# An MLP's value weights, loaded across the border of two column groups

## The chip, the core and the metric

The kernel runs on one core of a Trainium2 chip. The metric is the device time of one execution in microseconds (us). Before the change it is 1210.47 us, the median of three runs (1209.59 to 1212.47). TensorE (PE in the profile) multiplies matrices, VectorE (DVE) and ScalarE (ACT) work on elements, GpSimd (POOL) hardly matters here, and SyncE (SP) issues most of the loads from HBM.

## What is computed

Two layers of a decoder trunk on 512 tokens of width 1024, in float32. The first has sliding-window attention and a short gated convolution, the second gated linear attention; both end with the same gated MLP and a per-layer embedding. The change is in the MLP:

```python
D_MODEL, SEQ, D_FF, FFN_CONV_K = 1024, 512, 2816, 3
def _conv_ffn(h, w_up, conv_w, conv_b, w_down):
    u = _causal_depthwise_conv(h @ w_up, conv_w) + conv_b
    gate, up = jnp.split(u, 2, axis=-1)
    return (jax.nn.gelu(gate, approximate=False) * up) @ w_down
```

`w_up` has 2 x 2816 columns: the first half makes the gate, the second half the values that the gate multiplies.

## The kernel before

The matmuls run on pairs of numbers. Each float32 operand is split into a rounded part (`wh`, ScalarE) and the rest (`wl`, VectorE), and three products (lines 169 to 171, or 878 to 880) take the place of one. This split is called a cut: `cut` (lines 149 and 150) for plain weights, `cut_blocks` (lines 825 and 826) for weights that are used in blocks.

The up-projection `h @ w_up` of a layer runs in 11 groups. Group d makes two columns of 128 gate features and two columns of 128 value features, for all 512 tokens. The two halves are computed in different ways:

- The **gate columns** 256d to 256d + 255 go through `seven`: a scheme of seven half-size block products in the place of eight. Its weights are the plain blocks, sums and differences of blocks that VectorE forms in place in the loaded buffer (lines 849 to 860), each cut in turn. The last cut that reads the buffer is `last = self.cut_blocks(od)`. `seven` is a generator: each `next(steps)` issues some products and returns after a small copy between PSUM tiles, line 899 and line 902 among them.
- The **value columns** are plain products of three matmuls each (`value`, 48 matmuls a column), each with a cut of its own (`column`).

The weights come from HBM into two buffers of one pool (tag `raw`, 1 MB each, `bufs=2`). A load can only be issued when the cuts that read the buffer's former content are done. In `prepare(d)`, `loaded(d)` issues both loads of group d on SP's queue: first 256 value columns, then 256 gate columns. Then the second value column (`w1`) is cut, then the gate forms, and then the first value column.

TensorE's order is written out by hand. Group d begins with 36 matmuls of the column that was cut first (`begin`), goes on with products of the gate, mixed with the other value column (`V0`), and while its last gate products run, `prepare(d + 1)` is already recorded. Between L899 and L902 stands half a value column, and after L902 come the last two gate products, 24 matmuls, ahead of the next group. ScalarE and VectorE take their instructions in an order that a scheduler has fixed when the program was built, and each engine takes its own queue in that order. `tc.issue_after(x)` puts what is recorded inside it behind instruction x, where both are on one engine.

What VectorE does in a group besides the cuts: it scales the product by the tokens' norm (`z`, line 927, or 930 and 934) and adds two taps of the convolution (`zt`, line 937) for each of the four columns, and multiplies value and gate (line 982 or 992) after ScalarE's gelu (line 1077).

Of the kernel before, what the change touches and what calls it, by code (L numbers as in the profile page):

```python
# [19 lines left out]
P = 128  # L20
# [3 lines left out]
ND = D // P  # L24
DFF = 2816
NF = DFF // P
# [37 lines left out]
class Kernel:  # L64
# [291 lines left out]
    def project(self, load, ks, done, then):  # L356


        for m2 in range(0, ND, 2):
            pss = [self.ps(), self.ps()]  # L360
            raw = self.raw(ND, 2 * P)
            load(raw, slice(m2 * P, (m2 + 2) * P))
            w = self.cut(raw, "b")
            for c in range(2):
                for k in range(ND):
                    self.mm3(pss[c], w(k, c * P, (c + 1) * P), ks[k], start=k == 0, stop=k == ND - 1)
            if m2 + 2 == ND:
                then()
            for c in range(2):
                done(m2 + c, pss[c])  # L370
# [536 lines left out]
    def ffn(self, i, project, next_gain):  # L907


        nc, a, tc = self.nc, self.a, self.tc  # L910
        gain = self.g_ffn[i]
        wu = a["ffn_w_up"][i].rearrange("(k p) n -> p k n", p=P)
        w0, w1, w2, bb = self.fcv

        mine, other = (("a0", "a1"), ("b0", "b1"))[:: 1 - 2 * i]
        with tc.tile_pool(name=f"ffn{i}", bufs=1) as fp:
# [4 lines left out]
            def both():  # L921
                return fp.tile([P, 2, S], F32, tag="zt", name=self.nm("zt"), bufs=2)

            def taps(y, ps, f, more=None, behind=None):
                z = fp.tile([P, S], F32, tag="z", name=self.nm("z"), bufs=3)
                if more is None:
                    nc.vector.tensor_tensor(z, ps, R, ALU.mult)  # L927
                else:
                    h2 = lambda x: x.rearrange("p (u t) -> p u t", u=2)
                    nc.vector.tensor_tensor(  # L930
                        h2(z), h2(ps), more.unsqueeze(1).to_broadcast([P, 2, S // 2]), ALU.add
                    )
                    with tc.issue_after(behind.ins) if behind else nullcontext():
                        nc.vector.tensor_tensor(z, z, R, ALU.mult)  # L934
                nc.scalar.activation(y, z, AF.Identity, scale=w2[:, f : f + 1], bias=bb[:, f : f + 1])  # L935
                for tap, w in ((1, w1), (2, w0)):
                    nc.vector.scalar_tensor_tensor(  # L937
                        out=y[:, tap:], in0=z[:, : S - tap], scalar=w[:, f : f + 1], in1=y[:, tap:],
                        op0=ALU.mult, op1=ALU.add,
                    )  # L940

            def loaded(d):

                out = [self.raw(ND, 256) for _ in range(2)]
                for raw, c0 in zip(out, (DFF + 256 * d, 256 * d)):
                    nc.sync.dma_start(raw, wu[:, :, c0 : c0 + 256])
                return out

            def column(raw, c):
                return self.cut(raw[:, :, c * P : (c + 1) * P], "b", BLOCKS)  # L950

            def value(w, ps, k0, k1):
                for c, k in itertools.product(HALVES, range(k0, k1)):
                    self.mm3(
                        ps[:, c], w(k, 0, P), [x[:, c] for x in xg[k]], start=c.start == 0 and k == 0,
                        stop=k == ND - 1,
                        skip_group_check=True,
                    )

            def prepare(d):  # L960

                rv, rg = loaded(d)
                w1 = column(rv, 1)
                ev, od = self.by_parity(rg)
                ws = self.seven_forms(ev, od, rg)
                return self.seven(od, ws, xg, self.forms), w1, column(rv, 0)

            def begin(d, steps, w):

                ps = self.pa()  # L970
                value(w, ps, 0, 6)
                next(steps)
                value(w, ps, 6, ND)
                return lambda y: taps(y[:, 1], ps, NF + 2 * d + 1)

            def place(d, g, y):

                f = 2 * d
                if f < 8:
                    kept[f : f + 2] = [self.fp.tile([P, S], F32, tag=other[0], name=self.nm("u")) for _ in range(2)]  # L980
                    for u in range(2):
                        nc.vector.tensor_tensor(kept[f + u], g[:, u], y[:, u], ALU.mult)
                    return
                if d == groups - 1:
                    x = y
                else:
                    if f % 4 == 0:
                        fours.append(self.four(fp, F32))
                    x = fours[-1][:, f % 4 : f % 4 + 2]
                kept[f : f + 2] = [x[:, 0], x[:, 1]]  # L990
                pairs[f] = x
                nc.vector.tensor_tensor(x, g, y, ALU.mult)
# [3 lines left out]
            def split_one(f):  # L996

                tag = other[1 if f < 4 else 0]
                h = self.fp.tile([P, S], F32R, tag=tag, name=self.nm("uh"))
                pool, tag = (self.fp, tag) if f < 7 else (self.sp, "R")  # L1000
                acts[f] = h, pool.tile([P, S], F32R, tag=tag, name=self.nm("ul"))
                self.split(acts[f], kept[f])
# [6 lines left out]
            def split_acts():  # L1009
                for f in (6, 7):  # L1010
                    split_one(f)
# [24 lines left out]
            xg = self.xg  # L1036
            ready = []

            def done(m, ps):
                nc.vector.tensor_tensor(self.xT[m], self.xT[m], ps, ALU.add)  # L1040
                self.operand(m, gain, mine)

            project(done, lambda: ready.extend(prepare(0)))
            steps, w1c, w0c = ready
            with tc.manual_schedule(engines={ET.PE}):
                late = begin(0, steps, w1c)
                close = lambda: None
                for d in range(groups):
                    g, y = both(), both()
                    copied = next(steps)  # L1050
                    with tc.issue_after(copied.ins):
                        close()
                    V0 = self.pa()
                    value(w0c, V0, 0, ND // 2)
                    if d == 0:
                        self.end_norm()
                    copied = next(steps)
                    value(w0c, V0, ND // 2, ND)
                    if d == 0:
                        R = self.spread()  # L1060
                    X, Y, more = next(steps)
                    rest, cut = late, None

                    if d + 1 < groups:
                        steps, w1c, w0c = prepare(d + 1)
                        cut = self.rest_cut
                        late = begin(d + 1, steps, w1c)
                    else:
                        split_acts()
                    with tc.issue_after(copied.ins):  # L1070
                        rest(y)
                    taps(y[:, 0], V0, NF + 2 * d)
                    taps(g[:, 0], X, 2 * d)
                    taps(g[:, 1], Y, 2 * d + 1, more, cut)

                    def close(d=d, g=g, y=y):
                        nc.scalar.activation(g, g, AF.Gelu)
                        place(d, g, y)
                        if 4 <= d < groups - 1:
                            split_one(d - 4)  # L1080

                close()
# [910 lines left out]
```

## Time and profile before

| | us |
|---|---|
| median of the runs shown | 1210.47 (1209.59 to 1212.47) |
| the profiled execution, its own time | 1212.17 |
| its span in the profile | 1210.4 |
| up-projection of layer 0, groups 0 to 10 (first matmul to first of the down-projection) | 179.01 to 411.04 |
| up-projection of layer 1 | 802.69 to 1033.40 |

The times in a row of the profile are microseconds from the start of the span. A row in order of time has start, duration, engine, line, operation, output and inputs, shape; in brackets stands for how long the engine was idle before it and what ended that. A row of stretches begins with its bounds and its length, and gives each engine's busy time and instructions (PE, PEld, DVE, ACT, POOL), the granted clock, the share of the DMA engines and GB/s. A row of the chain has start, duration and what it was. The granted TensorE clock is 0.999 of full speed over the whole span.

### The profile page before, as it was taken

The numbers are of one execution on the slowest core, as the hardware profiler recorded it, in microseconds if no ns is written. First come the engines' busy times: TensorE is split into PE (matmuls) and PEld (weight loads), VectorE is DVE, ScalarE is ACT, GpSimd is POOL, SyncE is SP. The second block draws the span as 40 slices with busy tenths as digits, with TensorE's granted clock in tenths as the row PEclk, the third lists the DMA queues.
The fourth block names the chain that finished last, engine by engine and source line by source line (L and its number), as shares of the span: only waits on it lengthen the run. The fifth ranks groups of instructions, "written<-read, shape, count | busy, mean of one in ns | idle before, by whom it ended". The sixth has DMA issues, their size and how long they took to land.

```text
span 1210.4 us, 19832 instructions
## 1 busy us (share of the span) xinstructions
PE 1199.7 (99%) x8074; PEld 1080.0 (89%) x8074; DVE 968.3 (80%) x1543; ACT 667.0 (55%) x1093; POOL 45.1 (4%) x64
## 2 busy tenths in 40 slices
PE   9999999999999999999999999999999999999998
PEld 8877789999999989888988988899999999888887
DVE  6786687898998996746679876678988899988595
ACT  7466565655555744534563555555555656645374
POOL 2610000000000000000100000000000000000000
PEclk9999999999999999999999999999999999999999
DMA  7232222424233243222322222322242423422601
GB/s 221 72 103 72 73 70 71 139 70 137 73 102 108 88 140 96 96 100 82 114 93 69 73 69 70 105 78 98 72 139 70 138 72 110 137 94 96 209 1 70
DMA packets 111135, 117.74 MB, mean 97 GB/s; under 512 B 2840, under 2 KB 106322, under 8 KB 111044
## 3 DMA queue, kind: packets, MB, share of 16 engines
q1 hardware_dynamic: 109680, 115.35, 28.9%
q8 instruction: 63, 1.03, 0.4%
q0 software_dynamic: 560, 0.42, 0.3%
q10 hardware_dynamic: 804, 0.70, 0.2%
q14 instruction: 28, 0.23, 0.1%
HBM read 114.37 MB, written 2.10 MB: 96 GB/s over the span
## 4 chain that ended last, share of the span: by engine, by line
PE 63%; DVE 26%; DMA 7%; ACT 3%; issue 2%; ACTq 0%; DVEq 0%
PE ps L169 13%; PE ps L171 13%; PE ps L170 13%; DMA raw<-in_ffn_w_up_dram 7%; DVE zt L937 6%; DVE wl L826 5%; DVE wl L150 4%; PE ps L878 2%; PE pa L171 2%; PE pa L170 2%; PE ps L880 2%; PE ps L879 2%; PE pa L169 2%; DVE z L927 2%; PE ps L1390 1%
## 5 line engine op out<-in xcount | busy, mean ns | idle before, releaser
L149 ACT ACTIVATE wh<-raw 128x1024 fp32r<-128x1024 f32 (+4 forms) x154 | 152.3, 991 | 140.3 <-PE ps L170 90.4
L150 DVE TENSOR_TENSOR wl<-raw,wh 128x1024 fp32r<-128x1024 f32 (+4 forms) x154 | 175.4, 1140 | 62.9 <-ACT wh L149 61.2
L825 ACT ACTIVATE wh<-raw 128x1024 fp32r<-128x1024 f32 x78 | 82.9, 1063 | 104.7 <-DVE raw L850 67.8
L937 DVE SCALAR_TENSOR_TENSOR zt<-z,vfa,zt 128x510 f32<-128x510 f32 (+1 forms) x176 | 131.1, 746 | 0.8
L826 DVE TENSOR_TENSOR wl<-raw,wh 128x1024 fp32r<-128x1024 f32 x78 | 95.4, 1223 | 16.1 <-ACT wh L825 15.8
L171 PE MATMUL pa<-b,wl 128*128 128x256 f32 x352 | 98.1, 279 | 0.3
L171 PE MATMUL pa<-a,wl 128*128 128x256 f32 x352 | 98.0, 279 | 0.3
L169 PE MATMUL pa<-a,wh 128*128 128x256 f32 x352 | 97.3, 276 | 0.0
L170 PE MATMUL pa<-a,wh 128*128 128x256 f32 x352 | 97.2, 276 | 0.0
L169 PE MATMUL pa<-b,wh 128*128 128x256 f32 x352 | 97.2, 276 | 0.0
L170 PE MATMUL pa<-b,wh 128*128 128x256 f32 x352 | 97.2, 276 | 0.0
L935 ACT ACTIVATE zt<-z,vfb 128x512 f32<-128x512 f32 x88 | 71.4, 811 | 32.0 <-DVE z L934 20.7
L169 PE MATMUL ps<-b,wh 128*128 128x512 f32 x192 | 76.6, 399 | 0.0
L170 PE MATMUL ps<-b,wh 128*128 128x512 f32 x192 | 75.1, 391 | 0.0
L171 PE MATMUL ps<-b,wl 128*128 128x512 f32 x192 | 75.0, 390 | 0.0
L878 PE MATMUL ps<-four,wh 128*128 128x256 f32 x232 | 65.5, 283 | 3.1 <-ACT ps L902 2.9
L171 PEld LDWEIGHTS pa<-b,wl 128*128 128x128 f32 x352 | 66.1, 188 | 1.4 <-DVE wl L150 1.3
L171 PEld LDWEIGHTS pa<-a,wl 128*128 128x128 f32 x352 | 66.1, 188 | 1.2 <-DVE wl L150 1.0
L169 PEld LDWEIGHTS pa<-a,wh 128*128 128x128 f32 x352 | 66.1, 188 | 0.0
L169 PEld LDWEIGHTS pa<-b,wh 128*128 128x128 f32 x352 | 66.1, 188 | 0.0
L170 PEld LDWEIGHTS pa<-a,wh 128*128 128x128 f32 x352 | 66.1, 188 | 0.0
L170 PEld LDWEIGHTS pa<-b,wh 128*128 128x128 f32 x352 | 66.1, 188 | 0.0
(472 smaller groups left out, 3668.5 us busy)
## 6 DMA issues: line engine op xcount, KB each, us to landing
raw<-in_ffn_w_up_dram SPq DMA_DIRECT2D x44, 1024.0 KB, 5.3
raw<-in_ffn_w_down_dram SPq DMA_DIRECT2D x13, 1024.0 KB, 4.7
raw<-in_hy_w_in_dram SPq DMA_DIRECT2D x8, 1024.0 KB, 4.9
raw<-in_gla_w_in_dram SPq DMA_DIRECT2D x8, 1024.0 KB, 5.1
raw<-in_ffn_w_down_dram SPq DMA_DIRECT2D x8, 768.0 KB, 4.2
raw<-in_ple_w_gate_dram SPq DMA_DIRECT2D x6, 1024.0 KB, 4.6
raw<-in_hy_w_out_dram SPq DMA_DIRECT2D x16, 256.0 KB, 3.9
raw<-in_gla_w_out_dram SPq DMA_DIRECT2D x4, 1024.0 KB, 4.7
```

What stands on the lines that cost most here:

```text
L149: nc.scalar.activation(hv, v, AF.Copy)
L150: self.rest_cut = nc.vector.tensor_tensor(lv, v, hv.bitcast(F32), ALU.subtract)
L169: mm(out, lh, rh, start=start, stop=False, **kw)
L170: mm(out, lh, rl, start=False, stop=False, **kw)
L171: mm(out, ll, rh, start=False, stop=stop, **kw)
L825: nc.scalar.activation(h, src, AF.Copy)
L826: nc.vector.tensor_tensor(l, src, h.bitcast(F32), ALU.subtract)
L878: mm(out, wh, xh, start=first and j == 0, stop=False, **kw)
L879: mm(out, wh, xl, start=False, stop=False, **kw)
L880: mm(out, wl, xh, start=False, stop=j == ND // 2 - 1, **kw)
L935: nc.scalar.activation(y, z, AF.Identity, scale=w2[:, f : f + 1], bias=bb[:, f : f + 1])
L937: nc.vector.scalar_tensor_tensor(out=y[:, tap:], in0=z[:, : S - tap], scalar=w[:, f : f + 1], in1=y[:, tap:], op0=ALU.mult, op1=ALU.add,)
```

## The change

The columns of values are paired otherwise. Before, one load brought both value columns of a group. Now a load brings the second column of group d and the first column of group d + 1; the very first load of a layer brings one column alone (512 KB), and so does the last. In `prepare(d)` the first value column is cut from the load that was issued a group earlier, behind the instruction `copied` (the copy of line 902); then the gate load is issued; then the gate forms are cut; then the next value load is issued, and its first half, the second column of group d, is cut. The group begins with the first value column where it began with the second, so that `w0` and `w1` change places everywhere.

```diff
-            def loaded(d):
-                out = [self.raw(ND, 256) for _ in range(2)]
-                for raw, c0 in zip(out, (DFF + 256 * d, 256 * d)):
-                    nc.sync.dma_start(raw, wu[:, :, c0 : c0 + 256])
-                return out
+            def load_values(d):
+                c0, c1 = DFF + 256 * d + P, min(DFF + 256 * d + 3 * P, 2 * DFF)
+                if d < 0:
+                    c0 = DFF
+                raw = self.raw(ND, 256)[:, :, : c1 - c0]
+                nc.sync.dma_start(raw, wu[:, :, c0:c1])
+                return raw
...
-            def prepare(d):
-                rv, rg = loaded(d)
-                w1 = column(rv, 1)
+            values = []
+            def prepare(d, behind=None):
+                if d == 0:
+                    values.append(load_values(-1))
+                rv = values.pop()
+                with tc.issue_after(behind.ins) if behind else nullcontext():
+                    w0 = column(rv, rv.shape[2] // P - 1)
+                rg = self.raw(ND, 256)
+                nc.sync.dma_start(rg, wu[:, :, 256 * d : 256 * d + 256])
                 ev, od = self.by_parity(rg)
                 ws = self.seven_forms(ev, od, rg)
-                return self.seven(od, ws, xg, self.forms), w1, column(rv, 0)
+                values.append(load_values(d))
+                return self.seven(od, ws, xg, self.forms), w0, column(values[0], 0)
...
-                return lambda y: taps(y[:, 1], ps, NF + 2 * d + 1)
+                return lambda y: taps(y[:, 0], ps, NF + 2 * d)
...
-                        steps, w1c, w0c = prepare(d + 1)
+                        steps, w0c, w1c = prepare(d + 1, copied)
...
-                    taps(y[:, 0], V0, NF + 2 * d)
+                    taps(y[:, 1], V1, NF + 2 * d + 1)
```

TensorE's order is the same row for row, apart from the names of the operands. Three other places move.

The first is **ScalarE at the border of groups 6 and 7 of layer 0**. `zt_462` is the gate of group 5 before its gelu, `wh_502` the rounded value column with which group 7 begins, `raw_500` and `raw_501` the value and gate loads of group 7. Before:

```order
L108 ACTIVATE uh_495_3490<-u_350_2228 128x512
L1077 ACTIVATE zt_462_3193<-zt_462_3193 128x1024
L149 ACTIVATE wh_502_3588<-raw_500_3584 128x1024
L902 COPY ps_487_3399<-ps_486_3398 128x256
L935 ACTIVATE zt_493_3448<-z_517_3679,vfb_230_1430 128x512
L825 ACTIVATE wh_504_3592<-raw_501_3585 128x1024
```

Now (lines from 942 on have moved, by 10 at most: the gelu's 1077 is 1087; `raw_481` is the value load that was issued in group 6, `raw_503` the gate load of group 7):

```order
L108 ACTIVATE uh_496_3492<-u_351_2230 128x512
L1087 ACTIVATE zt_463_3195<-zt_463_3195 128x1024
L902 COPY ps_488_3401<-ps_487_3400 128x256
L149 ACTIVATE wh_501_3586<-raw_481_3355 128x1024
L935 ACTIVATE zt_494_3450<-z_518_3681,vfb_230_1430 128x512
L825 ACTIVATE wh_504_3592<-raw_503_3590 128x1024
```

The value cut and the copy of line 902 have changed places, and the cut reads a buffer that another load than the newest fills. The same holds at all other borders of groups.

The second is **VectorE at the same border**. `z_517` and `z_518` are the two value columns of group 6, scaled. Before:

```order
L992 TENSOR_TENSOR four_465_3235<-zt_462_3193,zt_463_3194 128x1024
L150 TENSOR_TENSOR wl_503_3589<-raw_500_3584,wh_502_3588 128x1024
L937 SCALAR_TENSOR_TENSOR zt_493_3448<-z_517_3679,vfa_227_1423,zt_493_3448 128x511
L937 SCALAR_TENSOR_TENSOR zt_493_3448<-z_517_3679,vfa_227_1423,zt_493_3448 128x510
L927 TENSOR_TENSOR z_518_3684<-pa_497_3494,R_324_2043 128x512
L826 TENSOR_TENSOR wl_505_3593<-raw_501_3585,wh_504_3592 128x1024
```

Now:

```order
L1002 TENSOR_TENSOR four_466_3237<-zt_463_3195,zt_464_3196 128x1024
L150 TENSOR_TENSOR wl_502_3587<-raw_481_3355,wh_501_3586 128x1024
L937 SCALAR_TENSOR_TENSOR zt_494_3450<-z_518_3681,vfa_227_1423,zt_494_3450 128x511
L927 TENSOR_TENSOR z_519_3686<-pa_498_3496,R_325_2045 128x512
L937 SCALAR_TENSOR_TENSOR zt_494_3450<-z_518_3681,vfa_227_1423,zt_494_3450 128x510
L826 TENSOR_TENSOR wl_505_3593<-raw_503_3590,wh_504_3592 128x1024
```

Here the scaling of line 927 has moved in between the two taps.

The third is **SP's queue in the first groups of layer 0**. Before, the loads stood in pairs of values and gate, group by group:

```order
L946 DMA raw_288_1795<-in_ffn_w_up_dram 128x8x256
L946 DMA raw_289_1796<-in_ffn_w_up_dram 128x8x256
L946 DMA raw_325_2069<-in_ffn_w_up_dram 128x8x256
L946 DMA raw_326_2070<-in_ffn_w_up_dram 128x8x256
L946 DMA raw_354_2321<-in_ffn_w_up_dram 128x8x256
```

Now a short value load comes first, and from then on gate (line 972) and values (line 948) alternate:

```order
L948 DMA raw_288_1795<-in_ffn_w_up_dram 128x8x128
L972 DMA raw_291_1801<-in_ffn_w_up_dram 128x8x256
L948 DMA raw_298_1819<-in_ffn_w_up_dram 128x8x256
L972 DMA raw_328_2075<-in_ffn_w_up_dram 128x8x256
L948 DMA raw_335_2093<-in_ffn_w_up_dram 128x8x256
```

Of a pair, the gate load now stands ahead of the values' one, and each waits for its own buffer: the gate load for the last cut of the gate before, the value load for the cut of the value column with which the next group begins.

ScalarE has one more swap in every group from 3 on: the copy of line 890 now stands ahead of the cut `t2` (line 825).

More of the change, by code (lines that the diff above doesn't have):

```diff
@@ L1043, in ffn @@
             project(done, lambda: ready.extend(prepare(0)))
-            steps, w1c, w0c = ready
+            steps, w0c, w1c = ready
             with tc.manual_schedule(engines={ET.PE}):
-                late = begin(0, steps, w1c)
+                late = begin(0, steps, w0c)
                 close = lambda: None
@@ L1052, in ffn @@
                         close()
-                    V0 = self.pa()
-                    value(w0c, V0, 0, ND // 2)
+                    V1 = self.pa()
+                    value(w1c, V1, 0, ND // 2)
                     if d == 0:
@@ L1057, in ffn @@
                     copied = next(steps)
-                    value(w0c, V0, ND // 2, ND)
+                    value(w1c, V1, ND // 2, ND)
                     if d == 0:
@@ L1064, in ffn @@
                     if d + 1 < groups:
-                        steps, w1c, w0c = prepare(d + 1)
+                        steps, w0c, w1c = prepare(d + 1, copied)
                         cut = self.rest_cut
-                        late = begin(d + 1, steps, w1c)
+                        late = begin(d + 1, steps, w0c)
                     else:
```

## The prediction

> **What bounds the kernel now.** I read the page's first part, the waits of TensorE, TensorE's order of time in the two up-projections, and then the chain that ended last. The first part seems to say that there is nothing to win, as TensorE (PE) is busy 99%:
>
> ```profile
> PE 1199.7 (99%) x8074; PEld 1080.0 (89%) x8074; DVE 968.3 (80%) x1543; ACT 667.0 (55%) x1093; POOL 45.1 (4%) x64
> raw<-in_ffn_w_up_dram SPq DMA_DIRECT2D x44, 1024.0 KB, 5.3
> ```
>
> But matmuls overlap in the trace (one of 256 columns shows 0.28 us and the next starts 0.11 us later), so a hole shorter than that is hidden in the busy time. I therefore measure from start to start. Every group of the up-projection begins with the same matmul, the first of `value(w, ps, 0, 6)`. Here it stands for groups 1, 2, 4, 6 and 10 of layer 0, and 2, 4 and 10 of layer 1:
>
> ```profile
> 200.38 0.28 PE L169 MATMUL pa<-a,wh 128*128 128x256 f32 x1
> 220.78 0.28 PE L169 MATMUL pa<-a,wh 128*128 128x256 f32 x1
> 262.04 0.28 PE L169 MATMUL pa<-a,wh 128*128 128x256 f32 x1
> 305.38 0.28 PE L169 MATMUL pa<-a,wh 128*128 128x256 f32 x1
> 390.50 0.28 PE L169 MATMUL pa<-a,wh 128*128 128x256 f32 x1
> 844.46 0.28 PE L169 MATMUL pa<-b,wh 128*128 128x256 f32 x1
> 885.70 0.28 PE L169 MATMUL pa<-b,wh 128*128 128x256 f32 x1
> 1012.88 0.28 PE L169 MATMUL pa<-b,wh 128*128 128x256 f32 x1
> ```
>
> Group 1 takes 220.78 - 200.38 = 20.40 us. It is the shortest, and I take it as what TensorE needs without a wait: 180 matmuls at 0.113 us are the same 20.4. The eight periods from group 2 to group 10 take 169.72 us in layer 0 and 168.42 in layer 1. At 20.40 each they would take 163.20. So **TensorE loses 6.52 + 5.22 = 11.74 us** in these sixteen periods, and that is the stock from which this change can draw.
>
> What takes it? The chain that ended last leaves TensorE in these groups and runs in a circle. From group 6 into group 7, and from 8 into 9:
>
> ```profile
> 317.07 1.15 DVE wl L826
> 318.22 0.02 issue
> 318.24 8.00 DMA raw<-in_ffn_w_up_dram
> ...
> 326.32 1.07 ACT wh L825
> 327.39 0.02 issue
> 327.41 1.22 DVE wl L826
> ...
> 360.70 7.21 DMA raw<-in_ffn_w_up_dram
> ...
> 369.09 1.23 DVE wl L826
> ```
>
> The reader is to see one loop: VectorE's last cut of a group's gate weights frees their `raw` buffer, the next gate load is issued, lands after 8.00 us, ScalarE rounds it (L825), VectorE subtracts (L826), and from there VectorE works without a pause until it frees the buffer again:
>
> ```profile
> 305.45 1.22 DVE L826 TENSOR_TENSOR wl<-raw,wh 128x1024 fp32r<-128x1024 f32 x1
> 305.45:320.14 14.69, 14.69 (x130) 14.62 (x130) 14.69 (x21) 7.75 (x12) 0.00 (x0) 1.00 0.17 53
> 347.91 1.22 DVE L826 TENSOR_TENSOR wl<-raw,wh 128x1024 fp32r<-128x1024 f32 x1
> ```
>
> From the cut at 305.45 to the issue at 318.24 are 12.79 us, and from the landing at 326.24 to the next cut 1.17. The loop is thus 13.96 us plus the load. With 8.00 that is 21.96, which is 327.41 - 305.45; with 7.21 it is 21.17, and 369.09 - 347.91 is 21.18. **Whenever the gate load takes over 6.44 us, this loop is longer than TensorE's 20.40**, and TensorE waits for its split weights.
>
> **Why the gate load is slow.** The value load of the same group is issued 1.7 us ahead of it (the value cut at 315.26 ends that much before the gate cut), so that two loads of 1 MB share the DMA engines. Alone, such a load is faster: the first two of layer 0 were issued 10.9 us apart.
>
> ```profile
> L946 SPq DMA_DIRECT2D raw<-in_ffn_w_up_dram x2: 367/367/367, 154.3 to 165.2; - x2
> DMA to landing us min/median/max: 5.2/5.3/5.4
> ```
>
> A second place of loss hangs on the same pair. ScalarE takes its queue in order, and the first cut of the next group's values stands ahead of a copy for which TensorE waits:
>
> ```profile
> 320.24 1.06 ACT L1077 ACTIVATE zt<-zt 128x1024 f32<-128x1024 f32 x1 [1.48 <-DVE zt L937]
> 322.45 1.06 ACT L149 ACTIVATE wh<-raw 128x1024 fp32r<-128x1024 f32 x1 [1.15 <-DMA raw<-in_ffn_w_up_dram]
> 323.41 0.37 ACT L902 COPY ps<-ps 128x256 f32<-128x256 f32 x1
> 323.83 0.38 PE L878 MATMUL ps<-four,wh 128*128 128x256 f32 x1 [0.43 <-ACT ps L902]
> PEld ps L878 <- ACT ps L902: 6.4, 11, 1.6
> ```
>
> **The change, part by part.**
>
> *Loads.* The bytes stay the same: of the 22 loads of 1 MB in a layer (44 in both) 21 stay so, and one becomes two halves. What moves is when they go out. The gate load still goes out when the last gate cut has freed its buffer. The value load now waits for the first cut of the next group, which stands behind the copy of L902: some 5.5 us later (the last gate cut starts at 317.07, the first value cut at 323.54 with its wait of 0.98). So the gate load is alone in its first 5 us. I take 5.3 us for it, the median of the two that were alone; the ends are 5.2 and the 8.00 of above, should the pair not be the reason. The loop is then 13.96 + 5.3 = 19.3 us, under 20.40, with 1.1 us to spare.
>
> The value load has time: it goes out about 2 us before the group starts, and its second column is cut nearly 10 us into the group (the cut at 315.26, group 6 starting at 305.38). A load of 8 us would still land in time. On SP's queue it stands behind a gate load that was issued 5.5 us before, and ahead of one that is not due for 14 us, so it holds up neither.
>
> *The first value cut.* It reads a column that landed a group ago, so it waits for no DMA, and it stands behind L902. By the rows above: the gelu (L1077) starts at 320.24, the next instruction can start 0.96 later (323.41 - 322.45 for an activation of that size), L902 runs at 321.20 instead of 323.41, and the cut at 321.50 instead of 322.45. L902 would be done at 321.57, well over 1 us before the matmul that waited until 323.83 could start at all, and its wait is gone. The wait that is added, the cut behind L902, holds up what is queued behind it on ScalarE (L935 and the gate cut L825): L825 could start at 321.50 + 0.96 + 0.81 = 323.3, and the gate load lands at 318.24 + 5.3 = 323.5. It holds up no matmul, as TensorE needs the value cut 24 matmuls, 2.7 us, after the one at 323.83.
>
> *VectorE.* When neither DMA nor TensorE is waited for, VectorE is next. Its own round is: 15.88 us from the gate cut to the product (305.45 to 321.33, by the rows below), then the value cut as soon as ScalarE has finished (321.50 + 1.06 + 0.03 = 322.59, or 17.14 into the round), then that cut, two taps and one scaling up to the next gate cut.
>
> ```profile
> 321.33 1.23 DVE L992 TENSOR_TENSOR four<-zt,zt 128x1024 f32<-128x1024 f32 x1 [1.19 <-ACT zt L1077]
> 323.54 1.23 DVE L150 TENSOR_TENSOR wl<-raw,wh 128x1024 fp32r<-128x1024 f32 x1 [0.98 <-ACT wh L149]
> 324.68 1.53 DVE L937 SCALAR_TENSOR_TENSOR zt<-z,vfa,zt 128x511 f32<-128x511 f32 x2
> 326.13 0.68 DVE L927 TENSOR_TENSOR z<-pa,R 128x512 f32<-128x512 f32 x1
> ```
>
> That last piece takes 327.41 - 323.54 - 0.60 of idle time, 3.2 to 3.3 us, so **the round is 17.14 + 3.2 = 20.3 us. TensorE's 20.40 is longer by a hair, and becomes the bound.** The swap of a tap and the scaling (L927 now between the two taps) is worth at most 0.1 us either way; I take nothing.
>
> *The sum.* The 11.74 us go, but for two things. Groups 2 and 3 lose 262.04 - 220.78 - 40.80 = 0.46 us in layer 0 and 0.44 in layer 1 while VectorE is still catching up from the start; the change does not touch its work there, so 0.90 stays. And as the round is so close to 20.40, I leave 0.2 for stray waits. **Saved: 11.74 - 0.90 - 0.2 = 10.6 us.** The profiled execution took 1212.17 us (span 1210.4), which is 1.7 above the median of the runs, so it would become 1201.6; from the median of 1210.47 the forecast is **1199.9 us**. The other edits I cost at nothing. The order of the two columns changes no instruction's size; the smaller first load of a layer lies beside TensorE's projection ahead of group 0; the copy of L890, now ahead of the cut `t2`, waits for a product that is older than that cut's input. Without that cover each would cost a group one activation at most, some 1 us.
>
> **A rule and the row.** The same sixteen periods by busy time:
>
> ```profile
> 220.78:390.50 169.72, 167.59 (x1442) 165.12 (x1441) 152.47 (x202) 93.14 (x133) 0.00 (x0) 1.00 0.30 100
> 844.46:1012.88 168.42, 166.68 (x1443) 164.71 (x1441) 152.57 (x202) 93.08 (x133) 0.00 (x0) 1.00 0.30 101
> ```
>
> By these, TensorE idles only 2.13 + 1.74 = 3.87 us, and no edit here could win more: the time would be 1206.6. The Trainium skill (Perfetto Trace Analysis, Identifying the Most-Contended Engine) says that matmul busy time is no good measure of the distance to the limit, since pipelined matmuls look otherwise in a trace. By that rule the starts count, not the busy time, and the starts here agree: 20.40 us was reached by a period whose matmuls are the same.
>
> **Rivals.**
>
> 1. *VectorE becomes the bound.* It has only 0.1 us in hand. For it: 152.5 us of work in 168.4, and the shortest round in the rows is 347.91 - 327.41 = 20.50. Were it 20.75, fourteen periods would lose 0.35 each, 4.9 us: 1204.6; at 20.9, 1206.7. Against it: that round of 20.50 still had a late load in it.
> 2. *Busy time is all there is*: 1206.6, as above. Against it stand the starts.
> 3. *The gain is given back.* After group 10 VectorE is the busiest, and TensorE just gets by:
>
> ```profile
> 1053.00:1063.00 10.00, 9.75 (x44) 7.72 (x42) 10.00 (x18) 6.17 (x9) 0.00 (x0) 1.00 0.32 105
> ```
>
> If VectorE comes no earlier into the down-projection, TensorE would wait there for what it won: about 1210, no change. Against it: VectorE's round shortens with TensorE's. This is also the case in which the change does not do what it says.
>
> 4. *Slower.* The place is the gate load. If it takes 8.00 us for a reason of its own, and not for its neighbour, the loop stays 21.96 in every period, as no early value column can help it: sixteen times 1.56 is 25.0 us lost instead of 11.74, so 1223.7. It decides from a load of 7.2 us up (16 x (13.96 + 7.17 - 20.40) = 11.7). Against it: 5.2 and 5.4 for those that were alone.
>
> **How the numbers follow.** Forecast 0.70; VectorE bound 0.13; busy time 0.05; given back 0.06; slower 0.05; the rest is better than forecast. The range goes down to 1197.5 (the 0.90, the 0.2 and the 0.25 of idle TensorE in the last row go too, and the fastest run before was 0.9 under its median) and up to 1206.5, which takes in most of rival 1. Under 0.2%, 2.4 us, a measurement of this kernel can't tell a change: faster 0.89, same 0.06, slower 0.05.
>
> **What would show it.** Right: groups start 20.4 to 20.5 us apart from group 4 on; the gate load lands 5.0 to 5.6 us after its issue; no load is named in ScalarE's waits for L825; TensorE's waits for L902 are gone. Rival 1: loads land early, yet groups are 20.6 or more apart and matmuls wait for `wl` or `t2`. Rival 4: loads of over 7 us without a neighbour. I would be wrong in the sum, too, if the value cut came late for TensorE, that is if the first matmuls of a group waited for L150.

## The result, and the profile after

The changed kernel takes 1201.27 us (median of 5 runs, 1200.52 to 1201.6). The kernel before, run beside it, takes 1211.98 us (5 runs, 1209.59 to 1212.47). The ratio is 0.9917 (0.9902 to 0.9931): **10.7 us less**. The profiled execution took 1201.25 us, with a span of 1199.4 (before 1212.17 and 1210.4) at a granted clock of 0.999.

The page of after, its first part, the shares of the chain, and the MLP's loads:

```profile
PE 1192.4 (99%) x8074; PEld 1076.9 (90%) x8074; DVE 966.4 (81%) x1543; ACT 671.1 (56%) x1093; POOL 44.8 (4%) x64
PE 92%; DVE 5%; ACT 1%; DMA 1%; issue 0%; ACTq 0%; DVEq 0%
raw<-in_ffn_w_up_dram SPq DMA_DIRECT2D x42, 1024.0 KB, 5.1
```

The chain of the kernel before had these shares:

```profile
PE 63%; DVE 26%; DMA 7%; ACT 3%; issue 2%; ACTq 0%; DVEq 0%
```

No engine's busy share has moved by more than a point, yet the chain has left VectorE and the loads and runs through TensorE nearly all the time. What the change did stands in the starts of the groups, in TensorE's order of time (groups 2, 4, 7 and 10 of layer 0; 2, 4 and 10 of layer 1):

```profile
220.54 0.28 PE L169 MATMUL pa<-a,wh 128*128 128x256 f32 x1
261.74 0.28 PE L169 MATMUL pa<-a,wh 128*128 128x256 f32 x1
322.94 0.28 PE L169 MATMUL pa<-a,wh 128*128 128x256 f32 x1
384.14 0.28 PE L169 MATMUL pa<-a,wh 128*128 128x256 f32 x1
837.94 0.28 PE L169 MATMUL pa<-b,wh 128*128 128x256 f32 x1
879.65 0.28 PE L169 MATMUL pa<-b,wh 128*128 128x256 f32 x1
1002.05 0.28 PE L169 MATMUL pa<-b,wh 128*128 128x256 f32 x1
```

From 261.74 to 384.14 are six periods of exactly 20.40 us, and so are the six from 879.65 to 1002.05. The sixteen periods lose 163.60 - 163.20 = 0.40 us in layer 0 and 164.11 - 163.20 = 0.91 in layer 1, where they lost 11.74. That is 10.43 of the 10.9 us by which the span is shorter (1210.39 before, 1199.45 now). The rest is small: 0.25 before group 0 of layer 0, some 0.15 between the layers, and 0.12 from the start of group 10 of layer 1 to the end (197.51 us before, 197.39 now). The two rows of busy time:

```profile
220.54:384.14 163.60, 163.60 (x1443) 163.50 (x1441) 152.19 (x203) 95.69 (x134) 0.00 (x0) 1.00 0.33 106
837.94:1002.05 164.11, 164.03 (x1442) 163.60 (x1441) 152.33 (x203) 95.34 (x134) 0.00 (x0) 1.00 0.33 106
```

VectorE does the same work in them as before (152.2 and 152.3 us against 152.5 and 152.6).

The gate loads from group 4 to group 10 of layer 0, as the view of their line (972) gives them: who waited for them (us, times), and their time to landing:

```profile
  ACT wh L825: 0.8, 1
DMA to landing us min/median/max: 4.8/5.0/5.9
```

And the border of groups 6 and 7, ScalarE first, then VectorE with the last gate cut of the round before, the value cut and the last gate cut:

```profile
316.57 1.06 ACT L1087 ACTIVATE zt<-zt 128x1024 f32<-128x1024 f32 x1 [1.48 <-DVE zt L937]
317.75 0.36 ACT L902 COPY ps<-ps 128x256 f32<-128x256 f32 x1
318.02 1.06 ACT L149 ACTIVATE wh<-raw 128x1024 fp32r<-128x1024 f32 x1
320.30 1.07 ACT L825 ACTIVATE wh<-raw 128x1024 fp32r<-128x1024 f32 x1 [0.52 <-PE pa L170]
```

```profile
301.78 1.22 DVE L826 TENSOR_TENSOR wl<-raw,wh 128x1024 fp32r<-128x1024 f32 x1
319.12 1.23 DVE L150 TENSOR_TENSOR wl<-raw,wh 128x1024 fp32r<-128x1024 f32 x1 [0.23 <-ACT wh L149]
322.18 1.22 DVE L826 TENSOR_TENSOR wl<-raw,wh 128x1024 fp32r<-128x1024 f32 x1
```

The gate cut of ScalarE (L825) no longer names a load in its brackets, but TensorE. VectorE's round is 322.18 - 301.78 = 20.40, the period of TensorE, and its cut now starts 0.76 us ahead of the group (322.18 against 322.94) where it started 0.07 behind it (305.45 against 305.38). TensorE leads.

### The profile page after: what moved, and what is told of

It is laid out like the page before. It is cut to its first block, busy times and chain, and to the rows that moved or that the text cites. A ratio compares the mean times of both kernels' runs of the same rounds, so it can differ in the third digit from the quotient of the medians.

```text
span 1199.4 us, 19840 instructions
## 1 busy us (share of the span) xinstructions
PE 1192.4 (99%) x8074; PEld 1076.9 (90%) x8074; DVE 966.4 (81%) x1543; ACT 671.1 (56%) x1093; POOL 44.8 (4%) x64
## 4 chain that ended last, share of the span: by engine, by line
PE 92%; DVE 5%; ACT 1%; DMA 1%; issue 0%; ACTq 0%; DVEq 0%
PE ps L169 14%; PE ps L170 14%; PE ps L171 14%; PE pa L170 7%; PE pa L171 7%; PE pa L169 7%; PE ps L878 5%; PE ps L880 5%; PE ps L879 5%; PE pa L878 2%; PE pa L880 2%; PE pa L879 2%; PE ps L1400 1%; PE ps L1398 1%; PE ps L1399 1%; DVE wl L150 1%
## 5 line engine op out<-in xcount | busy, mean ns | idle before, releaser
L149 ACT ACTIVATE wh<-raw 128x1024 fp32r<-128x1024 f32 (+4 forms) x154 | 152.5, 992 | 128.9 <-PE ps L170 92.8
L825 ACT ACTIVATE wh<-raw 128x1024 fp32r<-128x1024 f32 x78 | 83.0, 1064 | 115.8 <-DVE raw L850 75.9
```

What stands on the lines that cost most here:

```text
L149: nc.scalar.activation(hv, v, AF.Copy)
L825: nc.scalar.activation(h, src, AF.Copy)
```

## The experiments

Two theories stood against each other. **A**: the circle of the gate load (13.96 us plus the load) set the period, and the change wins because the gate load is no longer issued 1.74 us behind another one. **B**: what TensorE waited for was the copy of L902 behind a value cut that waits for its load. The first kernels (the copy first, the loads alone, the small neighbour, the short hold) ran beside 19 runs of the kernel before, with a median of 1210.84; the next four (both repeats, the long hold, the 128 columns) beside 9, at 1211.54; and the last three, with a single run each, beside one of 1211.54.

### 1. The copy first, and nothing else

The kernel before, with the value cut behind L902:

```diff
-            def prepare(d):
+            def prepare(d, behind=None):
...
-                w1 = column(rv, 1)
+                with tc.issue_after(behind.ins) if behind else nullcontext():
+                    w1 = column(rv, 1)
...
-                        steps, w1c, w0c = prepare(d + 1)
+                        steps, w1c, w0c = prepare(d + 1, copied)
```

> The kernel before, with its paired loads, but the first value cut of a group stands behind the copy of line 902. Theory A (the circle of buffer, gate load and VectorE sets the pace): TensorE's waits for the copy go, but the gate load still lands after 6 to 8 us, the groups still take 21 us on the mean, and the time stays at 1209 to 1212 us. Theory B (the copy that is queued behind a waiting cut is the cause): 4.6 to 6.4 us are won, 1205 to 1207 us.

Measured: 1210.03 us (10 runs, 1207.15 to 1212.46), ratio 0.9999 (0.9986 to 1.0012). No change. The profiled execution is the fastest of the ten (1207.15 us). TensorE's matmuls wait for the copy no more in it; weight loads wait 2.3 us in all, as in the kernel after the change. The chain shows one whole circle:

```profile
303.09 1.23 DVE wl L826
...
315.88 6.52 DMA raw<-in_ffn_w_up_dram
...
322.49 1.07 ACT wh L825
...
323.58 1.23 DVE wl L826
```

From cut to issue 12.79, the load 6.52, from landing to cut 1.18: 20.49 us in all, as A's formula has it. With the copy out of the way the load sets the period just the same. B falls. The circle after this one runs through the value load (issued at 334.64, landed 5.11 us later), behind whose cut VectorE's other work is queued, so that the gate load is not the only load that counts in this kernel.

### 2. The loads alone

The changed kernel without its rule of order. ScalarE then does the value cut ahead of L902 again:

```diff
-                        steps, w0c, w1c = prepare(d + 1, copied)
+                        steps, w0c, w1c = prepare(d + 1)
```

> The changed kernel without the rule that puts the first value cut behind the copy of line 902; the cut stands ahead of the copy again, as in the kernel before. Theory A: its data landed a group ago, so the copy comes 1 us later and is still in time; 1200.5 to 1202.5 us. Theory B: TensorE waits for the copy again, 4.6 us are lost, about 1206 us.

Measured: 1200.34 us (4 runs), ratio 0.9912 (0.9896 to 0.9929). ScalarE at the border of groups 6 and 7:

```profile
317.90 1.04 ACT L149 ACTIVATE wh<-raw 128x1024 fp32r<-128x1024 f32 x1
318.84 0.37 ACT L902 COPY ps<-ps 128x256 f32<-128x256 f32 x1
```

The order of before is back, and costs nothing: the cut reads a column that landed long ago and waits for no load, so L902 is some 1 us later, and TensorE had that in hand. The pair was run once more against the whole change on another chip.

The whole change:

> The changed kernel once more, beside the next run on the same chip: 1200 to 1202 us.

The loads alone:

> The changed kernel without the rule that puts the first value cut behind the copy of line 902, once more. Theory A (the rule is worth nothing): within 0.1% of the run of the changed kernel beside it. Rival (the rule keeps the copy in time now and then): 1 to 3 us slower than that.

Measured: 1200.61 us (5 runs), ratio 0.9916 (0.9902 to 0.9929), and 1200.33 us (4 runs), ratio 0.991 (0.9896 to 0.9923). The rule behind `copied` makes no difference that these runs can tell.

### 3. The kernel before with a small neighbour

The value load brings one block of the eight (128 KB), and the cuts use it for all:

```diff
-                for raw, c0 in zip(out, (DFF + 256 * d, 256 * d)):
-                    nc.sync.dma_start(raw, wu[:, :, c0 : c0 + 256])
+                nc.sync.dma_start(out[0][:, :1], wu[:, :1, DFF + 256 * d : DFF + 256 * d + 256])
+                nc.sync.dma_start(out[1], wu[:, :, 256 * d : 256 * d + 256])
+                out[0] = out[0][:, :1].to_broadcast([P, ND, 256])
```

> The kernel before, but a value load brings one eighth of its weights (128 KB), which serves for all eight blocks, so that the values are wrong; cuts and matmuls are as many and as large as before. Theory A: the gate load has the DMA engines nearly to itself, lands 5.0 to 5.4 us after its issue, groups take 20.4 to 20.6 us, the time is 1200.5 to 1204 us. Rival (the gate load is slow for a reason of its own): it stays at 6 to 8 us and the time at 1209 to 1212 us.

Measured: 1200.06 us (4 runs), ratio 0.991 (0.9893 to 0.9926). The gate loads of groups 4 to 10 of layer 0:

```profile
DMA to landing us min/median/max: 4.7/4.8/6.3
```

They go out 1.74 to 1.94 us behind the value load, nearly as close as ever, and take 4.8 us where those of before took 6.2 to 8.2 (the five of these groups whose landing the trace has). From group 4 on the groups are 20.40 us apart. With the order unchanged and only the neighbour made small, the whole gain is there: the gate load was slow because of its neighbour. One thing this run leaves open is the value load, which lands earlier too; the pair of runs in section 5 settles it.

### 4. Holding the gate load back

Two runs give the changed kernel its circle back by holding the gate load: a write of one column into its buffer, so that the load must wait for it. In the first, VectorE writes behind a split (line 109):

```diff
-            nc.vector.tensor_tensor(l, src, h.bitcast(F32), ALU.subtract)
+            self.low = nc.vector.tensor_tensor(l, src, h.bitcast(F32), ALU.subtract)
...
-            values = []
+            values, held = [], []
...
+                if held:
+                    with tc.issue_after(held.pop().ins):
+                        nc.vector.tensor_copy(rg[:, 0, :1], self.ones[:, :1])
...
                             split_one(d - 4)
+                            held.append(self.low)
```

> The changed kernel, with the gate load of groups 6 to 10 (both layers) held back by some 1.4 us, until VectorE has done the split of line 109. Theory A: the circle becomes 13.96 + 1.4 + 5.0 = 20.4 us, just TensorE's own period, so 1201 to 1203.5 us. Rival (the loop has no slack, each held microsecond is paid): ten borders by 1.4 us, about 1215 us.

Measured: 1207.35 us (10 runs, 1205.53 to 1209.04), ratio 0.9969 (0.9956 to 0.9982). Both numbers were missed, and the trace says why: the write (L974) came a tap later than I had reckoned. VectorE from the last gate cut on, then the chain from one gate cut to the next:

```profile
335.37 1.22 DVE L826 TENSOR_TENSOR wl<-raw,wh 128x1024 fp32r<-128x1024 f32 x1
...
338.44 0.15 DVE L974 COPY raw<-ones 128x1 f32<-128x1 f32 x1
```

```profile
323.82 1.23 DVE wl L826
...
338.65 4.87 DMA raw<-in_ffn_w_up_dram
...
344.70 1.23 DVE wl L826
```

The load went out 14.83 us behind the first cut, 2.04 later than without the hold. 13.96 + 2.04 + 4.87 is 20.87, and the two cuts are 20.88 apart. The dose was wrong, the formula held.

In the second ScalarE writes behind the value cut, far later:

```diff
+                if behind:
+                    with tc.issue_after(behind.ins):
+                        nc.scalar.copy(rg[:, 0, :1], self.ones[:, :1])
```

> The changed kernel, with every gate load held back until ScalarE has done the copy of line 902 and the first value cut, some 4.7 us after its buffer is free. Theory A: the circle becomes 13.96 + 4.7 + 5.0 = 23.7 us, groups 1 to 10 of each layer take 23 to 24 us, and some 18 periods by 3.3 us are lost: 1250 to 1270 us. Rival (what counts is that the two loads are apart, not when the gate load goes out): under 1210 us.

Measured: 1252.79 us (one run), in the expected range. The ten groups 1 to 10 of layer 0 take 22.1 to 24.8 us, 23.2 on the mean: of the delay, forecast at 4.7 us, the circle's slack takes a part, and 2.8 us are lost in a group on the mean. This run showed something else too: here the value load is the second of the pair, 1.2 us behind the gate load. For groups 4 to 10 of layer 0, the view of the gate loads' line, then that of the value loads' line:

```profile
DMA to landing us min/median/max: 5.0/5.1/6.0
```

```profile
DMA to landing us min/median/max: 7.4/8.0/8.2
```

Now the value load is the slow one. Whichever load of the pair goes second pays; the first pays next to nothing (5.1 us in the median, 5.0 in the changed kernel).

### 5. What the second load pays for

In the kernel before, the 16 DMA engines have no time to spare behind the gate load's issue. The rows of stretches, with the engines' share (1 is full) and GB/s at the end: first 5.26 us from the issue of a gate load of the kernel before (the one that took 8.00), then the 3.2 us in which a lone gate load of the changed kernel moves its data:

```profile
318.24:323.50 5.26, 5.17 (x46) 4.97 (x44) 3.13 (x4) 2.63 (x4) 0.00 (x0) 1.00 1.04 354
```

```profile
356.40:359.60 3.20, 3.20 (x31) 3.20 (x30) 2.01 (x3) 2.11 (x3) 0.00 (x0) 1.00 0.98 323
```

So the two loads do share the engines. If that were the whole price, half the bytes in the first should halve it. The kernel before, with value loads of 128 columns (512 KB), used for both columns:

```diff
-                for raw, c0 in zip(out, (DFF + 256 * d, 256 * d)):
-                    nc.sync.dma_start(raw, wu[:, :, c0 : c0 + 256])
+                nc.sync.dma_start(out[0][:, :, P:], wu[:, :, DFF + 256 * d + P : DFF + 256 * d + 256])
+                nc.sync.dma_start(out[1], wu[:, :, 256 * d : 256 * d + 256])
...
-                return self.seven(od, ws, xg, self.forms), w1, column(rv, 0)
+                return self.seven(od, ws, xg, self.forms), w1, column(rv, 1)
```

> The kernel before, but a value load brings 128 columns (512 KB), which serve as both value columns of the group, so that the values are wrong; cuts and matmuls are as before. Theory A (the gate load waits its turn behind the bytes that are ahead of it): it lands 0.5 to 1.5 us earlier than before, at 5.0 to 5.8 us, the circle falls under 20.40 us and the time is 1200 to 1204 us. Rival (any neighbour delays it in full): 6 to 8 us as before, 1209 to 1212 us.

Measured: 1209.18 us (one run), the rival's number; the periods from group 4 to group 10 of layer 0 are 20.57 to 21.33 us. The gate loads of groups 4 to 10 of layer 0:

```profile
DMA to landing us min/median/max: 6.6/6.7/7.4
```

So it is not the bytes alone. Nor are the engines full here: between the two loads (gate load issued at 337.42) they are half idle:

```profile
338.70:339.50 0.80, 0.80 (x10) 0.80 (x9) 0.63 (x1) 0.08 (x1) 0.00 (x0) 1.00 0.51 134
```

Such a load brings 512 bytes of each of 1024 rows, as many pieces as before. The next run brings the same 512 KB in 512 pieces of 1 KB, four blocks of 256 columns, in the place of the two lines removed above:

```diff
+                half = out[0][:, : ND // 2]
+                nc.sync.dma_start(half, wu[:, : ND // 2, DFF + 256 * d : DFF + 256 * d + 256])
+                nc.sync.dma_start(out[1], wu[:, :, 256 * d : 256 * d + 256])
+                out[0] = half.rearrange("p k (c n) -> p (k c) n", c=2)
...
-                w1 = column(rv, 1)
+                w1 = column(rv, 0)
```

> The kernel before, but a value load brings 4 blocks of 256 columns (512 KB in pieces of 1 KB) and both value columns are made from these: half of the value weights is left out. In the run with half the columns (512 KB in pieces of 512 bytes, as many pieces as before) the gate load still took 6.5 to 7.4 us. Theory 'pieces' (what delays the gate load is the number of pieces ahead of it, 1024 before and there, 128 in the run with one block, here 512): gate load 5.3 to 6.2 us from group 4 on, periods 20.4 to 20.6, 1200.5 to 1204. Theory 'in flight' (any load that is still moving some 2 us after the gate load's issue makes it slow, whatever its size): 6.5 to 7.4 us, periods 20.5 to 21.4, 1207 to 1210.

Measured: 1201.46 us (one run); the starts of groups 4 to 10 are 20.40 us apart in both layers. The gate loads:

```profile
DMA to landing us min/median/max: 5.6/5.8/6.8
```

SP's queue (packets, MB, share of the 16 engines) in the pages of the kernel before, of the 128 columns and of the four blocks:

```profile
q1 hardware_dynamic: 109680, 115.35, 28.9%
```

```profile
q1 hardware_dynamic: 109680, 103.82, 26.8%
```

```profile
q1 hardware_dynamic: 98416, 103.82, 27.0%
```

The last two move the same bytes. The one has 11264 packets less, 512 for each of the 22 value loads, and its gate load is 0.9 us faster. The value load itself lands early in both (3.7 and 3.5 us in the median), so that it is the gate load that parts 1209 from 1201 us. By pieces ahead of it, the gate load takes 4.8 us (128), 5.8 (512) and 6.7 (1024 of 512 bytes), and 6.2 to 8.2 in the kernel before (1024 of 1 KB). The number fits all four. Between the two runs of 512 KB the size of a piece changes with the number, so that these two alone do not part the one from the other.

The Trainium skill (DMA: Bandwidth & Descriptors, Why small descriptors are slow) has a fixed price of about three bus cycles for each packet beside one cycle for 32 bytes. By it the two halves cost 1024 x 19 = 19456 and 512 x 35 = 17920 cycles, 9% apart, an estimate; the runs have 6.7 - 4.8 = 1.9 against 5.8 - 4.8 = 1.0 us of delay, so that this price alone does not explain what the second load pays.

Two more runs change the distance and the queue. First the distance: VectorE writes one column into the gate's buffer ahead of each gate load.

```diff
                 for raw, c0 in zip(out, (DFF + 256 * d, 256 * d)):
+                    if c0 == 256 * d:
+                        nc.vector.tensor_copy(raw[:, 0, :1], self.ones[:, :1])
                     nc.sync.dma_start(raw, wu[:, :, c0 : c0 + 256])
```

> The kernel before, with a write of one column into the gate's buffer by VectorE ahead of each gate load, which VectorE does some 2 us after the last gate cut: the gate load is issued about 4 us behind the value load where it was 1.74, the bytes are the same. If only a close neighbour makes the gate load slow: 4.8 to 5.4 us, period 13.96 + 2.0 + 5.0 = 20.9 to 21.0, 16 x 0.55 = 8.8 us lost where 11.74 were, 1206 to 1210. If any neighbour within the value load's 5 us does: 6.2 to 8.2 us, periods of 22.2 to 24, 1230 to 1260.

Measured: 1213.23 us (one run). The chain from one gate cut to the next:

```profile
325.40 1.23 DVE wl L826
...
340.23 4.73 DMA raw<-in_ffn_w_up_dram
...
346.15 1.23 DVE wl L826
```

The value load ahead of it went out at 336.46, 3.77 us before, and the gate load takes 4.73 us with all the bytes and pieces of before. The circle is 13.96 + 2.04 + 4.73 = 20.73, measured 20.75. Of the five gate loads of groups 4 to 10 in layer 0 whose landing the trace has, three are as expected (4.7 to 5.2 us), two took 5.8 and 6.3. The time is over the range and no better than before, as some periods are 21.7 to 22.6 and not 20.9. Two can be followed in the trace: the group from 324.13 to 345.92 has a gate load of 5.76, and the one that ends at 388.93 a value load of 6.41 with no neighbour near.

So much distance was not needed. In groups 1 to 3 of the kernel before itself the gate load goes out 2.60 to 3.06 us behind the value load, and takes 4.9 to 5.3 us in the five cases whose landing the trace has. The one at 190.99, 2.60 us behind:

```profile
DMA to landing us min/median/max: 5.3/5.3/5.3
```

Only the pairs 1.74 us apart, from group 4 on, are slow.

Then the queue: the gate loads from GpSimd's, the value loads from SP's as before.

```diff
-                for raw, c0 in zip(out, (DFF + 256 * d, 256 * d)):
-                    nc.sync.dma_start(raw, wu[:, :, c0 : c0 + 256])
+                for q, raw, c0 in zip((nc.sync, nc.gpsimd), out, (DFF + 256 * d, 256 * d)):
+                    q.dma_start(raw, wu[:, :, c0 : c0 + 256])
```

> The kernel before, with the gate loads issued by GpSimd on its own queue and the value loads left on SP's. If the second load is slow because both stand in SP's queue: gate load 4.8 to 5.5 us plus what GpSimd needs to start one, 1200 to 1205. If the 16 DMA engines are what they share: 6.2 to 8.2 us or more, periods over 20.5, 1208 to 1225.

Measured: 1210.04 us (one run). The view of GpSimd's loads, all 22 first, then the first one of layer 1, whose value load went out 11 us before:

```profile
L946 POOL DMA_DIRECT2D raw<-in_ffn_w_up_dram x22: 884/884/935, 164.6 to 1002.4; - x22
...
DMA to landing us min/median/max: 5.6/5.8/7.5
```

```profile
DMA to landing us min/median/max: 5.8/5.8/5.8
```

The load behind a close neighbour is now, in the median, as fast as the one without. That looks like a verdict for SP's queue and against the 16 engines, but it is none. The load goes out 2.0 us behind its neighbour and not 1.74, and it starts to move later still. The view of the DMA queues for the 1.95 us behind the issue of one of GpSimd's loads (336.95 to 338.90) has packets of SP's queue alone, and the engines full:

```profile
q1 hardware_dynamic: 701, 0.72, 104.6%
```

The value load had been issued at 334.94, so that some 4 us lay between its issue and the first packet of the gate load; on SP's queue a lone load's first packet comes 1.04 us after its issue. The run thus widened the distance too, which takes the price away on one queue as well. It does not tell the queue from the engines. The whole is hardly faster than before: some loads take 6.6 to 7.5 us, and of the six periods from group 4 to group 10 of layer 0 four are 20.40, but the two whose gate load took 6.80 and 6.56 are 21.06 and 21.16. What the second load pays for beside the full engines stays open.

Not tried: a third `raw` buffer, which should take the load out of the circle, and the gate load put first in the pair without a hold.

## Why the prediction was right

**The bound.** Right. The starts gave 11.74 us of stock, 10.43 of it are gone, and the period stands at 20.40 to the hundredth. The rival "busy time is all there is" could have given 3.87 us at most; 10.9 came. The Trainium skill (Perfetto Trace Analysis, Identifying the Most-Contended Engine), named there, calls the busy time of matmuls no good measure, and the trace agrees. That the starts are the better one is the prediction's own step, and the runs bear it out.

**The gate load.** The mechanism is right: the circle of 13.96 us plus the load fits the run with the copy first (20.49 measured, 13.96 + 6.52 = 20.48), the short hold (20.88 and 20.87) and the distance (20.75 and 20.73). The size was 5.3 us and is 5.0 in the median of groups 4 to 10, so the circle has some 1.4 us to spare (20.40 - 13.96 - 5.0) and not 1.1. Half right was the half sentence on why the load is slow, "two loads of 1 MB share the DMA engines". They do: the engines were full for 5.26 us behind its issue. But it is not the whole price, as halving the neighbour's bytes left 6.7 us with the engines half idle between the loads; fewer pieces ahead, or 2.6 us of distance, took most or all of the delay away. For this change it made no difference, as it puts 5.1 to 6.4 us between a value load and the gate load ahead of it, and 14.5 us and more between that and the next gate load.

**The first value cut and L902.** The rows came as worked out: the copy right behind the gelu, the cut behind the copy. TensorE's row of waits for this copy in the profile of before,

```profile
PE ps L878 <- ACT ps L902: 2.9, 4, 1.4
```

has no successor after. Only weight loads still wait for it, up to 0.4 us, ahead of matmuls that go on:

```profile
PEld ps L878 <- ACT ps L902: 2.3, 6, 0.4
```

Yet it was no loss of its own: putting the copy first in the kernel before won nothing, and letting the cut stand ahead after the change lost nothing. I had called it "a second place of loss" that hangs on the pair; it was the same loss, seen where TensorE happened to stand when the late load reached it.

**VectorE's round.** I had 20.3 us, a hair under TensorE's. It showed no period of its own: VectorE waits 1.19 us for the gelu and 0.23 for the cut, and runs 0.76 us ahead of the group. Rival 1 did not come.

**What stays.** I left 0.90 us for groups 2 and 3, and 0.2 for strays. There are 0.40 us in layer 0, and 0.91 in layer 1, 0.57 of it in one period of 20.97, which has its own cause in the chain:

```profile
851.71 6.25 DMA raw<-in_ffn_w_up_dram
858.04 1.08 ACT wh L825
859.14 1.23 DVE wl L826
```

A gate load with no other load issued near ahead of it (the next value load went out at 856.85) took 6.25 us. A packet of 16 KB from another queue, listed as `instruction`, was among its own:

```profile
q8 instruction: 1, 0.02, 0.9%
```

The circle was also longer in that early group, with 13.30 us from the cut at 838.41 to the issue where later groups have 12.79. Together 1.31 against 1.10.

**Given back later** did not come either: from group 10 of layer 1 on the span is 0.12 us shorter, not longer.

**The sum.** 10.6 us forecast. 10.43 came out of the sixteen periods, some 0.5 from the small terms that I had at nothing, 10.9 in the profiled executions. The two errors, 0.2 too much and 0.5 left out, cancel in part; so much of the agreement is luck. The profiled execution was put at 1201.6 and is 1201.25. The forecast of 1199.9 is 1.4 below the measured median because it started from a median of 1210.47 for the kernel before, which in the runs beside the change was 1211.98; from there it would have been 1201.4.

## What to carry to other kernels

Look for circles, not for shares: a buffer set free by the last step of a round, the load that it lets go, and the steps back to the release add up to a period, and if this is longer than the busiest engine's own, every microsecond of the load counts once a round. Measure that engine's period from start to start of the same instruction, since overlapping instructions hide the holes. When a load in such a circle is slow, look at what its queue was given just before: sending the neighbour 5 us later was worth as much here as making it eight times smaller.

## What the runs showed that I had not expected

- Of two loads of 1 MB 1.2 to 1.7 us apart on one queue the second pays: 6.2 to 8.6 us against some 5 for one by itself, while the first takes 5.0 to 6.0 in layer 0 of the kernel before. With 2.6 us between them, half of the first one's own 5 us, the price is mostly gone (5.3).
- The price does not go by the bytes of the first load alone: 512 KB cost the second 1.9 us in 1024 pieces and 1.0 in 512, one profiled execution each.
- A load without a neighbour takes 4.8 to 5.1 us most times, but now and then 5.8 to 7.2, in several of the kernels. The traces show what goes with it: of the loads of 1 MB of `w_up` on SP's queue with no other within some 5 us, every one that took 5.5 us or more had a 16 KB packet of the queue q8 (`instruction`) on an engine while its own packets moved, and none without such a packet took as long, though many with one were not slow. No run tests this. With 1.4 us to spare in the circle most of these stay hidden.
- A program's order can differ where the time does not: the rule that puts the cut behind the copy is worth nothing that 8 runs without it, on two chips, can tell.
